# Sixty low-part subtractions change their engine, the weight stream is read further ahead, and two one-hot tables are made earlier in a two-layer decoder kernel

## The chip, the cores and the metric

The kernel runs on one core of one Trainium2 chip. The metric is the device time of one execution in microseconds (us): the median of three runs before the change is 1326.42 us (1326.4 to 1328.45). The core has five engines with queues of their own, each of which works through its instructions in order: TensorE (PE, whose weight loads the profile lists as PEld), VectorE (DVE), ScalarE (ACT), GpSimd (POOL) and SyncE (SP, which here only issues DMAs).

## The reference

The kernel computes two decoder layers on 512 tokens of width 1024. Each layer has a mixer, a cross-attention into 256 memory tokens, and a mixture of 16 experts (hidden width 512), each followed by a layer norm. The change lies in the mixture, cut here to what matters:

```python
def grouped_moe(x, router_w, router_bias, w_gate, w_up, w_down):
    scores = softmax(x @ router_w)                    # 512 x 16
    ...                                               # best of 4 groups, two experts in it
    combine = sum(one_hot(expert_idx) * weights)      # 512 x 16, two entries a token
    y = zeros
    for e in range(16):
        he = silu(x @ w_gate[e]) * (x @ w_up[e])      # 1024 -> 512
        y = y + combine[:, e:e + 1] * (he @ w_down[e])  # 512 -> 1024
    return y

x = layer_norm(ALPHA * x + grouped_moe(x, ...), ln3_g, ln3_b)   # once per layer
```

## The kernel before

**Products in three parts.** Every fp32 number that goes into a product is cut into a high part (rounded to a shorter format) and a low part, the rest. A product is then three matmuls into one PSUM bank: high x high, high x low, low x high (`mm3`, lines 284 to 287, in this order L285, L286, L287). The last of the three needs the low part of the stationary operand, the second the low part of the weights.

**The weight stream.** All weights pass through one stream `W` of 488 pieces of 512 KB. A piece is loaded by a DMA that SP issues (`raw`, L133), ACT copies its high part (`whi`, L153), and then DVE or POOL subtracts: `wlo` = `raw` - `whi` (L156). `on_pool` is the set of pieces whose subtraction stands in POOL's queue. `raw`, `whi`, `wlo` and nearly every other large tile come from one pool of 44 units of 4 KB a partition, which are taken in turn as they come free. `prepare` splits pieces up to MOE_LOOK = 4 ahead of the product that uses them; `pump` issues loads up to `depth` pieces ahead of the split (MOE_DEPTH, an entry for each layer). Inside the expert loops a load also waits until an earlier piece has been split ("a piece is loaded as one is split"), and at most four loads are under way (IN_FLIGHT). Before the loop, beside the router, `moe` issues GATE_DEPTH pieces ahead.

**The expert loops.** An expert has 12 pieces: four of the gate matrix, four of the down matrix, four of the up matrix; the stream holds gate of e+1, down of e, up of e+1. For each expert at most 128 rows of tokens are gathered (`fetch`, a POOL indirect DMA). In one turn e of the loop (L1104 on): DVE forms `h` = silu(gate) x up (L1110); in even turns up to e = 12 DVE makes one-hot tables `r_oh` (L976) for the experts three and four on; PE runs the 24 matmuls of the gate of e+1, and after k = 3 of its eight steps turns `h` (L1117), which ACT (L261) and DVE (L262) split into `hT`, high and low; PE runs the 24 matmuls of the down matrix, with `hT` stationary; `index_of` sums one-hot tables on PE into row numbers (L995, reduced by DVE in L1000 to L1004); ACT scales the result into `ye` (L1149), POOL adds it into DRAM by a scattering DMA (`store`, L1037), and `ye`'s unit is free when that DMA has landed; then the up matrix of e+1. In the last turn of layer 0, DVE makes half of `ye` (L1147); the next layer norm reads the sum back (L1243). In layer 1, the table `oh` of expert 15 (L983), its four transposes (L987) and the ACT copy `back` (L989) are made in turn 9 (TURN_AT) between the store and the up products.

**What sets the order.** The loops stand under a manual schedule for PE, ACT and DVE: these three queues hold the instructions in the order in which the code is written. So a DVE instruction that waits holds up every one written after it. POOL and SP are ordered by the scheduler.

Of the kernel before, what the change touches and what calls it, by code (L numbers as in the profile page):

```python
# [26 lines left out]
NE = 16  # L27
# [6 lines left out]
UNITS = 44  # L34
MM_BANKS = 4
DEPTH = 4
MOE_DEPTH = {"l0_": 16, "l1_": 21}
SHARED = [None, None, False, False]
STAT1 = "VVVA"
BIAS1 = "PPPV"  # L40
TURN_AT = 9
# [2 lines left out]
PLOOK = 1  # L44
NORM_FROM = 4
IN_FLIGHT = 4
GATE_DEPTH = {"l0_": 18, "l1_": 24}
LAST_AHEAD = 1
POOL_W_SPLITS = 2
XO_DEPTH = {"l0_": 18, "l1_": 22}  # L50
# [25 lines left out]
def kernel(ctx: ExitStack, tc: tile.TileContext, I, out, stop=None):  # L76
# [14 lines left out]
    def unit(shape, dt=F32, name="u"):  # L91
        return units.tile(shape, dt, name=name, tag="u")
# [4 lines left out]
    def tpt(name="tp"):  # L97
        return tpp.tile([128, 4, 128], F32, name=name, tag="tp")
# [78 lines left out]
    W = Stream()  # L177
# [32 lines left out]
    plan()  # L210
    first, end = W.span["pool_w"]
    W.on_pool.update(range(first, first + POOL_W_SPLITS))
    for p in ("l0_", "l1_"):
        for e in range(NE - 1):
            W.on_pool.update((W.span[(p, "d", e)][0] + 1, W.span[(p, "u", e + 1)][0]))


    ident = consts.tile([128, 128], F32, name="ident")
# [641 lines left out]
    class Router:  # L860
# [116 lines left out]
                              pos.to_broadcast([128, NT, 128]), op=ALU.is_equal)  # L977
            return oh

        def slots_to_tokens(self, e):  # L980

            oh = unit([128, NT, 128], name="oh")
            vec.tensor_tensor(oh, self.tb.slot[:, None, :].to_broadcast([128, NT, 128]),  # L983
                              self.pos[:, :, e:e + 1].to_broadcast([128, NT, 128]), op=ALU.is_equal)
            tp = tpt()
            for t in range(NT):
                transpose(tp[:, t], oh[:, t], ident)  # L987
            back = unit([128, NT, 128], F32R, name="back")
            act(back, tp, AF.Copy)  # L989
            return back  # L990
# [50 lines left out]
    def expert_rows(w, xT, jobs={}):  # L1041

        ps = mmt()
        for k in range(KC):
            mm3(ps, xT.hi(k), xT.lo(k), *w[k], k == 0, k == KC - 1)
            if k in jobs:
                jobs[k]()
        return ps
# [41 lines left out]
    def experts(r, xT, groups, fetch, turn_part, turned, keep):  # L1090
        p = r.p
        half = lambda n: slice(n * 512, (n + 1) * 512)
        g_ps = expert_rows(W.take((p, "g", 0)), xT)
        r.index([2])
        fetch(2)

        def gate_of():
# [6 lines left out]
        for e in range(NE):  # L1104
# [4 lines left out]
            cur = made["x"]  # L1109
            mul = vec.tensor_tensor(h, h, u_ps, op=ALU.mult)  # L1110
            ohs = [r.one_hot(r.pos[:, :, i:i + 1]) for i in groups.get(e, [])]
            hT = unit([128, 2, 4, 128], F32R, name="hT")

            def turn_h():
# [17 lines left out]
            if not last or not keep:  # L1132
                if e + 2 < NE:
                    made["x"] = Split(128, "xgT")
                for k in range(4):
                    for n in range(2):
                        end = product(n, k)
                    if k == 0 and not last:
                        made["h"] = gate_of()
                    if k == 2 and e + 2 < NE:  # L1140
                        turn_part(e + 2, made["x"], 0)
                if e in groups:
                    r.index_of(groups[e], ohs)
                ye = unit([128, D], name="ye")
                for n in range(2):
                    if n and last:
                        vec.tensor_scalar_mul(ye[:, half(n)], acc[n], scale)  # L1147
                    else:
                        ev = act(ye[:, half(n)], acc[n], AF.Copy, scale=scale)  # L1149
                st = r.store(ye, r.idx[:, e:e + 1])  # L1150
                r.last = [mul, end, ev, st]
                if last:
                    W.after = st
                if e == NE - 2 and keep:
                    ln = Norm(I[p + "ln3_g"], I[p + "ln3_b"])
                    for t in range(NT):
                        nc.gpsimd.dma_start(X[t], r.y_dram[tok(t)])
            else:
                r.yh, r.yl = (unit([128, 2, 512], F32R, name="ye" + i) for i in "hl")
                for n in range(2):  # L1160
                    for k in range(4):
                        end = product(n, k)
                    ev = act(r.yh[:, n], acc[n], AF.Copy, scale=scale)
                    lo = vec.scalar_tensor_tensor(r.yl[:, n], acc[n], scale, r.yh[:, n].bitcast(F32),
                                                  op0=ALU.mult, op1=ALU.subtract)
                r.last = [mul, end, ev, lo, st]
            if not last:
                if e + 3 < NE:
                    fetch(e + 3)
                if e == TURN_AT and keep:  # L1170
                    r.back = r.slots_to_tokens(NE - 1)
                if e == NE - 2:
                    W.last_ahead = W.span[(p, "d", NE - 1)][0] + LAST_AHEAD
                more = {1: lambda: turn_part(e + 2, made["x"], 1)} if e + 2 < NE else {}
                u_ps = expert_rows(W.take((p, "u", e + 1)), cur, more)
# [104 lines left out]
    for layer in range(2):  # L1280
        p = f"l{layer}_"
# [19 lines left out]
        r = Router(p, tb)  # L1301
# [6 lines left out]
        if stop == p + "ln2":  # L1308
            return finish()
        W.depth, W.look = MOE_DEPTH[p], MOE_LOOK  # L1310
        if layer == 0:
# [60 lines left out]
```

## Time and profile before

| | |
|---|---|
| median of three runs | 1326.42 us (1326.4 to 1328.45) |
| profiled execution: its own time, its span | 1327.66 us, 1325.5 us |
| PE, PEld busy | 94%, 79% |
| DVE, ACT, POOL busy | 76%, 58%, 26% |
| expert loop of layer 0 | 404.5 to 684.4 us of the span |
| expert loop of layer 1 | 1008.3 to 1293.2 us of the span |

Busy shares are of the whole span. The numbers of the argument come from stretches, above all the two expert loops. Where a matmul of 128 x 512 has nothing to wait for, the next one starts 0.23 us after it, though each is listed with 0.39 us, since matmuls overlap; so an idle gap of PE in a list of waits is some 0.16 us shorter than the delay between two starts.

### The profile page before, as it was taken

The numbers are of one execution on the slowest core, as the hardware profiler recorded it, in microseconds if no ns is written. First come the engines' busy times: TensorE is split into PE (matmuls) and PEld (weight loads), VectorE is DVE, ScalarE is ACT, GpSimd is POOL, SyncE is SP. The second block draws the span as 40 slices with busy tenths as digits, with TensorE's granted clock in tenths as the row PEclk, the third lists the DMA queues.
The fourth block names the chain that finished last, engine by engine and source line by source line (L and its number), as shares of the span: only waits on it lengthen the run. The fifth ranks groups of instructions, "written<-read, shape, count | busy, mean of one in ns | idle before, by whom it ended". The sixth has DMA issues, their size and how long they took to land. (4 is left out here: it accounts for less than half of the span.)

```text
span 1325.5 us, 18662 instructions
## 1 busy us (share of the span) xinstructions
PE 1248.0 (94%) x6680; PEld 1041.1 (79%) x6680; DVE 1009.3 (76%) x1422; ACT 767.9 (58%) x1143; POOL 347.4 (26%) x231
## 2 busy tenths in 40 slices
PE   7999999999989999999998979999969999989995
PEld 6878989888877777787776868988857778777873
DVE  4784746575769999998876666647659999998985
ACT  4665602463447887778774333246228778777873
POOL 2010001000104544544431320100013344443443
PEclk9999999999989999999999989999969999999999
DMA  9113513247538999999997242207546999999963
GB/s 319 49 49 112 183 56 96 80 143 271 207 107 306 339 354 329 335 347 347 355 356 252 83 139 84 80 17 281 180 155 224 320 355 352 336 354 354 341 223 147
DMA packets 133666, 298.81 MB, mean 225 GB/s; under 512 B 13819, under 2 KB 15883, under 8 KB 133568
## 3 DMA queue, kind: packets, MB, share of 16 engines
q1 hardware_dynamic: 118528, 260.08, 55.0%
q0 software_dynamic: 12160, 27.01, 7.4%
q10 hardware_dynamic: 2880, 10.49, 2.0%
q8 instruction: 53, 0.87, 0.3%
q14 instruction: 45, 0.37, 0.1%
HBM read 287.40 MB, written 26.74 MB: 237 GB/s over the span
## 5 line engine op out<-in xcount | busy, mean ns | idle before, releaser
L156 DVE TENSOR_TENSOR wlo<-raw,whi 128x1024 fp32r<-128x1024 f32 x426 | 576.3, 1391 | 86.9 <-ACT whi L153 64.4
L153 ACT ACTIVATE whi<-raw 128x1024 fp32r<-128x1024 f32 x488 | 488.0, 1058 | 80.8 <-PE mm L286 26.0
L156 POOL TENSOR_TENSOR wlo<-raw,whi 128x1024 fp32r<-128x1024 f32 x62 | 168.0, 2710 | 200.1 <-ACT whi L153 155.5
L285 PE MATMUL mm<-whi,xgTh 128*128 128x512 f32 x512 | 207.7, 406 | 0.0
L286 PE MATMUL mm<-wlo,xgTh 128*128 128x512 f32 x512 | 200.3, 391 | 1.2 <-POOL wlo L156 1.2
L287 PE MATMUL mm<-whi,xgTl 128*128 128x512 f32 x512 | 200.9, 392 | 0.0
L287 PEld LDWEIGHTS mm<-whi,xgTl 128*128 128x128 f32 x512 | 96.5, 188 | 21.4 <-DVE xgTl L262 0.2
L286 PEld LDWEIGHTS mm<-wlo,xgTh 128*128 128x128 f32 x512 | 96.9, 189 | 19.6 <-POOL wlo L156 1.7
L285 PEld LDWEIGHTS mm<-whi,xgTh 128*128 128x128 f32 x512 | 96.7, 189 | 17.6 <-ACT xgTh L261 0.2
L286 PE MATMUL mm<-wlo,hT 128*128 128x512 f32 x256 | 102.7, 401 | 6.4 <-DVE wlo L156 6.2
L349 POOL TENSOR_TENSOR ln_rs<-ln_rs,half_neg 128x1 f32<-128x1 f32 x24 | 31.9, 1331 | 284.0 <-DVE ln_rs L348 284.0
L285 PE MATMUL mm<-whi,hT 128*128 128x512 f32 x256 | 102.6, 401 | 1.4 <-ACT hT L261 1.4
L287 PE MATMUL mm<-whi,hT 128*128 128x512 f32 x256 | 101.9, 398 | 1.3
L1037 POOL DMA_INDIRECT l_y<-ye,r_idx x31 | 65.8, 2122 | 127.9 <-ACT ye L1149 95.7
L261 ACT ACTIVATE xgTh<-tp 128x512 fp32r<-128x512 f32 x64 | 38.2, 600 | 67.3 <-PE tp L271 67.2
L271 PE MATMUL tp<-ident,x 128*128 128x128 f32 x384 | 58.0, 285 | 16.6 <-DMA x<-in_x_dram 6.8
L271 PEld LDWEIGHTS tp<-ident,x 128*128 128x128 f32 x384 | 48.4, 146 | 27.6 <-issue 11.4
L286 PEld LDWEIGHTS mm<-wlo,hT 128*128 128x128 f32 x256 | 48.1, 188 | 24.7 <-DVE wlo L156 16.2
L261 ACT ACTIVATE x1Th<-tp 128x256 fp32r<-128x256 f32 x32 | 12.1, 384 | 86.5 <-PE tp L271 75.9
L285 PE MATMUL mm<-x1Th,whi 128*128 128x256 f32 (+1 forms) x192 | 60.7, 321 | 0.7 <-DVE xqTl L262 0.7
L286 PE MATMUL mm<-x1Tl,whi 128*128 128x256 f32 (+1 forms) x192 | 60.9, 318 | 0.0
L287 PE MATMUL mm<-x1Th,wlo 128*128 128x256 f32 (+1 forms) x192 | 60.9, 318 | 0.0
(328 smaller groups left out, 2616.4 us busy)
## 6 DMA issues: line engine op xcount, KB each, us to landing
raw<-in_l_e_gate_dram SPq DMA_DIRECT2D x128, 512.0 KB
raw<-in_l_e_up_dram SPq DMA_DIRECT2D x128, 512.0 KB
raw<-in_l_e_down_dram SPq DMA_DIRECT2D x128, 512.0 KB
raw<-in_l_xkv_dram SPq DMA_DIRECT2D x32, 512.0 KB
raw<-in_l_w_in_dram SPq DMA_DIRECT2D x22, 512.0 KB
raw<-in_l_w_out_dram SPq DMA_DIRECT2D x16, 512.0 KB
raw<-in_l_xq_dram SPq DMA_DIRECT2D x16, 512.0 KB
raw<-in_l_xo_dram SPq DMA_DIRECT2D x16, 512.0 KB
```

The costliest lines, as they stand in the source:

```text
L153: first = act(hi, raw, AF.Copy)
L156: self.last_split = [first, eng.tensor_sub(lo, raw, hi.bitcast(F32))]
L261: act(hi, src, AF.Copy)
L271: transpose(tp[:, j], rows(c0 + j), ident)
L285: mm(ps, sh, mh, start=first, stop=False)
L286: mm(ps, sh, ml, start=False, stop=False)
L287: return mm(ps, sl, mh, start=False, stop=last)
L349: nc.gpsimd.tensor_tensor(rs[:, 1:2], rs[:, 0:1], half_neg[:, 0:1], op=ALU.pow)
L1037: return nc.gpsimd.indirect_dma_start(out=self.y_dram[:], out_offset=bass.IndirectOffsetOnAxis(ap=idx, axis=0), in_=ye, in_offset=None, bo ...
```

## The change

Four edits. First, the loop that puts two pieces of each expert (the second of down, the first of up) into `on_pool` goes; their 30 subtractions in each loop then stand in DVE's queue, and POOL keeps its DMAs there. Second, MOE_DEPTH of layer 0 goes from 16 to 19 (with the piece being split that is 20 pieces ahead; layer 1 stays at 22), and GATE_DEPTH from 18 and 24 to 24 and 26. Third, the one-hot table for expert 2 is made before the first gate products, and only its sums stay behind them. Fourth, in turn 9 of layer 1 `oh` is made right after `h`, and its transposes and `back` follow the down products; the order on PE stays.

```diff
-MOE_DEPTH = {"l0_": 16, "l1_": 21}
+MOE_DEPTH = {"l0_": 19, "l1_": 21}
-GATE_DEPTH = {"l0_": 18, "l1_": 24}
+GATE_DEPTH = {"l0_": 24, "l1_": 26}
...
     W.on_pool.update(range(first, first + POOL_W_SPLITS))
-    for p in ("l0_", "l1_"):
-        for e in range(NE - 1):
-            W.on_pool.update((W.span[(p, "d", e)][0] + 1, W.span[(p, "u", e + 1)][0]))
...
-        def slots_to_tokens(self, e):
+        def slots(self, e):
             oh = unit([128, NT, 128], name="oh")
             vec.tensor_tensor(oh, ...)
+            return oh
+
+        def to_tokens(self, oh):
             tp = tpt()
...
+        ohs = [r.one_hot(r.pos[:, :, 2:3])]
         g_ps = expert_rows(W.take((p, "g", 0)), xT)
-        r.index([2])
+        r.index_of([2], ohs)
...
             ohs = [r.one_hot(r.pos[:, :, i:i + 1]) for i in groups.get(e, [])]
+            if e == TURN_AT and keep:
+                oh = r.slots(NE - 1)
             hT = unit([128, 2, 4, 128], F32R, name="hT")
...
                 if e in groups:
                     r.index_of(groups[e], ohs)
+                if e == TURN_AT and keep:
+                    r.back = r.to_tokens(oh)
                 ye = unit([128, D], name="ye")
...
-                if e == TURN_AT and keep:
-                    r.back = r.slots_to_tokens(NE - 1)
```

The order on PE and SP is the same before and after. DVE gains 60 subtractions, POOL loses them.

The first place is DVE in the loop of layer 0, from `h` of one turn with one-hot tables to the low part `hT` and what follows; the waits are those that each instruction carries (DMAHW: a load, DMASW: a DMA that POOL issued, Activation: ACT). Before:

```order
L1110 TENSOR_TENSOR h<-h,mm 128x512 [waits DMASW2_49,PE_49]
L976 TENSOR_TENSOR r_oh<-slot,r_pos 128x512 x2
L156 TENSOR_TENSOR wlo<-raw,whi 128x1024 [waits DMAHW6_49,Activation_49]
L262 TENSOR_TENSOR hT<-tp,hT 128x512 [waits Activation_49]
L156 TENSOR_TENSOR wlo<-raw,whi 128x1024 [waits DMAHW0_49,Activation_49]
L156 TENSOR_TENSOR wlo<-raw,whi 128x1024 [waits DMAHW1_49,Activation_49]
L156 TENSOR_TENSOR wlo<-raw,whi 128x1024 [waits DMAHW3_49,DMAHW7_49,Activation_49,Pool_49]
```

And after, in the same turn:

```order
L1112 TENSOR_TENSOR h<-h,mm 128x512 [waits PE_49]
L973 TENSOR_TENSOR r_oh<-slot,r_pos 128x512 x2
L156 TENSOR_TENSOR wlo<-raw,whi 128x1024 [waits DMAHW6_49,Activation_49]
L156 TENSOR_TENSOR wlo<-raw,whi 128x1024 [waits DMAHW7_49,DMASW1_49,Activation_49]
L259 TENSOR_TENSOR hT<-tp,hT 128x512 [waits DVE_49,Activation_49]
L156 TENSOR_TENSOR wlo<-raw,whi 128x1024 [waits DMAHW0_49,Activation_49]
L156 TENSOR_TENSOR wlo<-raw,whi 128x1024 [waits DMAHW1_49,DVE_49,Activation_49]
```

The second down piece has come in ahead of `hT`, and it carries the wait DMASW1: its `wlo` takes the unit of the `ye` of the turn before, which the scattering store still reads. Before, the unit went to a `whi` on ACT that stands behind `hT`:

```order
L261 ACTIVATE hT<-tp 128x512 [waits DVE_49,PE_49]
L153 ACTIVATE whi<-raw 128x1024 [waits DMAHW4_49,DMASW2_49]
L153 ACTIVATE whi<-raw 128x1024 [waits DMAHW5_49,DVE_49]
L153 ACTIVATE whi<-raw 128x1024 [waits DMAHW6_49,DVE_49]
L1099 ACTIVATE h<-mm 128x512 [waits DVE_49,PE_49]
```

These rows of before show ACT in such a turn, where the first `whi` behind `hT` waits for the store (DMASW2).

The second place is DVE in turn 9 of layer 1, from `h` to the table `oh`, before:

```order
L1110 TENSOR_TENSOR h<-h,mm 128x512
L156 TENSOR_TENSOR wlo<-raw,whi 128x1024
L262 TENSOR_TENSOR hT<-tp,hT 128x512
L156 TENSOR_TENSOR wlo<-raw,whi 128x1024 x4
L262 TENSOR_TENSOR xgTl<-tp,xgTh 128x512
L156 TENSOR_TENSOR wlo<-raw,whi 128x1024
L983 TENSOR_TENSOR oh<-slot,r_pos 128x512
```

And after:

```order
L1112 TENSOR_TENSOR h<-h,mm 128x512
L980 TENSOR_TENSOR oh<-slot,r_pos 128x512
L156 TENSOR_TENSOR wlo<-raw,whi 128x1024 x2
L259 TENSOR_TENSOR hT<-tp,hT 128x512
L156 TENSOR_TENSOR wlo<-raw,whi 128x1024 x5
```

`oh` has moved ahead of six subtractions and of `hT`.

The third place is DVE at the start of the loop of layer 0, where `r_oh` is the table of expert 2, before:

```order
L1004 TENSOR_REDUCE r_ws<-idx 128x1 x2
L262 TENSOR_TENSOR xgTl<-tp,xgTh 128x512 x2
L156 TENSOR_TENSOR wlo<-raw,whi 128x1024 x9
L976 TENSOR_TENSOR r_oh<-slot,r_pos 128x512
L1000 TENSOR_REDUCE r_row<-idx 128x1
```

And after:

```order
L1005 TENSOR_REDUCE r_ws<-idx 128x1 x2
L973 TENSOR_TENSOR r_oh<-slot,r_pos 128x512
L259 TENSOR_TENSOR xgTl<-tp,xgTh 128x512 x2
L156 TENSOR_TENSOR wlo<-raw,whi 128x1024 x9
L1001 TENSOR_REDUCE r_row<-idx 128x1
```

The table stood behind nine subtractions and now stands ahead of them.

## Rows read from the trace of the kernel before

**Rows 1.** The head of the profile page: span and engines.

```profile
span 1325.5 us, 18662 instructions
PE 1248.0 (94%) x6680; PEld 1041.1 (79%) x6680; DVE 1009.3 (76%) x1422; ACT 767.9 (58%) x1143; POOL 347.4 (26%) x231
```

**Rows 2.** Stretches of the span: its bounds and length, busy time of PE, PEld, DVE, ACT and POOL with the number of instructions, granted PE clock (1.00 is 2.4 GHz), DMA share, GB/s. The two expert loops, then a part of each, then the end of the first loop.

```profile
404.50:684.40 279.90, 273.01 (x1305) 218.85 (x1305) 258.50 (x242) 219.68 (x265) 132.97 (x60) 1.00 0.97 341
1008.30:1293.20 284.90, 276.15 (x1310) 220.43 (x1308) 270.20 (x243) 217.17 (x266) 124.81 (x60) 0.99 0.93 326
420.00:600.00 180.00, 178.04 (x855) 143.56 (x854) 171.78 (x161) 143.81 (x175) 88.10 (x40) 1.00 0.97 342
1010.00:1190.00 180.00, 175.84 (x846) 140.29 (x844) 176.46 (x159) 140.33 (x173) 80.47 (x39) 1.00 0.96 337
585.00:684.00 99.00, 94.58 (x446) 75.71 (x444) 84.04 (x82) 76.22 (x91) 45.83 (x21) 1.00 0.99 355
```

**Rows 3.** Groups of DVE instructions (count, busy us, mean ns of one, idle time before them), in three stretches: 20 to 380 us, where POOL has next to no subtraction, then 420 to 600 us, then 1010 to 1190 us.

```profile
L156 DVE TENSOR_TENSOR wlo<-raw,whi 128x1024 fp32r<-128x1024 f32 x58 | 68.9, 1220 | 22.3 <-ACT whi L153 15.2 <-issue 7.0
...
L156 DVE TENSOR_TENSOR wlo<-raw,whi 128x1024 fp32r<-128x1024 f32 x98 | 139.4, 1460 | 8.1 <-issue 4.2 <-ACT whi L153 3.9
...
L156 DVE TENSOR_TENSOR wlo<-raw,whi 128x1024 fp32r<-128x1024 f32 x95 | 140.3, 1513 | 3.4 <-ACT whi L153 2.3 <-issue 1.1
```

**Rows 4.** Two source lines: durations in ns (least, median, most), first and last start in us. The one-hot tables over the whole span, POOL's subtractions of the first loop.

```profile
L976 DVE TENSOR_TENSOR r_oh<-slot,r_pos x32: 677/686/2807, 376.1 to 1240.4; 128x512 bf16<-128x512 f32 x32
...
L156 POOL TENSOR_TENSOR wlo<-raw,whi x30: 2373/2683/3477, 406.1 to 675.4; 128x1024 fp32r<-128x1024 f32 x30
```

**Rows 5.** Timeline of turn 2 of the loop of layer 1 (start us, length us, engine, line, idle time before it in brackets): DVE's two tables together, POOL's subtraction beside them, and PE's first and seventh product of the down matrix.

```profile
1047.27 3.02 DVE L976 TENSOR_TENSOR r_oh<-slot,r_pos 128x512 bf16<-128x512 f32 x2
...
1046.75 2.39 POOL L156 TENSOR_TENSOR wlo<-raw,whi 128x1024 fp32r<-128x1024 f32 x1 [3.72 <-DVE wlo L156]
...
1050.85 0.39 PE L285 MATMUL mm<-whi,hT 128*128 128x512 f32 x1
1051.49 0.50 PE L286 MATMUL mm<-wlo,hT 128*128 128x512 f32 x1 [0.25 <-DVE wlo L156]
1052.09 0.50 PE L287 MATMUL mm<-whi,hT 128*128 128x512 f32 x1
...
1054.50 0.39 PE L285 MATMUL mm<-whi,hT 128*128 128x512 f32 x1
1055.33 0.50 PE L286 MATMUL mm<-wlo,hT 128*128 128x512 f32 x1 [0.44 <-DVE wlo L156]
```

**Rows 6.** The same place on PE in turn 2 of the loop of layer 0.

```profile
447.07 0.39 PE L285 MATMUL mm<-whi,hT 128*128 128x512 f32 x1
447.81 0.50 PE L286 MATMUL mm<-wlo,hT 128*128 128x512 f32 x1 [0.36 <-DVE wlo L156]
448.42 0.50 PE L287 MATMUL mm<-whi,hT 128*128 128x512 f32 x1
```

**Rows 7.** PE at the sums of expert 2's table in layer 0 and in layer 1, and at the transposes of `oh`; then the stretch behind these in the columns of rows 2.

```profile
397.95 0.25 PE L995 MATMUL idx<-tokv,r_oh 128*128 128x5 bf16 x4 [1.23 <-DVE r_oh L976]
...
1001.70 0.25 PE L995 MATMUL idx<-tokv,r_oh 128*128 128x5 bf16 x4 [1.91 <-DVE r_oh L976]
...
1192.01 0.63 PE L987 MATMUL tp<-ident,oh 128*128 128x128 f32 x4 [2.83 <-DVE oh L983]
...
1192.50:1196.00 3.50, 3.50 (x13) 2.87 (x12) 1.23 (x1) 1.61 (x3) 0.25 (x1) 0.53 0.98 322
```

**Rows 8.** The end of the first loop (585 to 684 us): ACT's copies as a group, and, earlier, SP's loads (start us, length us) beside the router of layer 0.

```profile
L153 ACT ACTIVATE whi<-raw 128x1024 fp32r<-128x1024 f32 x61 | 62.8, 1061 | 15.5 <-DMA l_y<-ye,r_idx 7.3 <-DMA raw<-in_l_e_up_dram 4.5 <-DMA raw<-in_l_e_down_dram 3.3
...
352.60 38.68 SPq L133 DMA_DIRECT2D raw<-in_l_e_up_dram  x4
392.03 4.81 SPq L133 DMA_DIRECT2D raw<-in_l_e_gate_dram  x4
```

**Rows 9.** The scattering store: ACT's copies behind `hT` in turns 2 and 6 of the first loop, the first down product of turn 6, and the line of the store with the time its DMAs take to land and who waited for it.

```profile
446.11 2.96 ACT L153 ACTIVATE whi<-raw 128x1024 fp32r<-128x1024 f32 x3 [0.99 <-DMA l_y<-ye,r_idx]
...
520.94 2.96 ACT L153 ACTIVATE whi<-raw 128x1024 fp32r<-128x1024 f32 x3 [1.91 <-DMA l_y<-ye,r_idx]
...
520.98 0.39 PE L285 MATMUL mm<-whi,hT 128*128 128x512 f32 x1
...
521.58 0.68 DVE L262 TENSOR_TENSOR hT<-tp,hT 128x512 fp32r<-128x512 f32 x1
...
  ACT whi L153: 17.5, 13
...
DMA to landing us min/median/max: 6.8/9.3/10.7
```

**Rows 10.** From the last product of the first loop to the read-back of its sum.

```profile
691.77 0.39 PE L287 MATMUL mm<-whi,hT 128*128 128x512 f32 x1
...
694.27 1.06 ACT L153 ACTIVATE whi<-raw 128x1024 fp32r<-128x1024 f32 x1 [2.89 <-DMA raw<-in_l_xkv_dram]
...
696.51 0.74 DVE L1147 TENSOR_SCALAR ye<-mm,r_ws 128x512 f32<-128x512 f32 x1
...
704.85 2.00 ACTq L1243 DMA_DIRECT2D x<-l_y  x4
```

**Rows 11.** The second loop's stream: ACT's copies from 1045 to 1265 us as a group.

```profile
L153 ACT ACTIVATE whi<-raw 128x1024 fp32r<-128x1024 f32 x137 | 136.1, 1059 | 3.0 <-DMA l_y<-ye,r_idx 3.0
```

## The prediction

> **What bounds the kernel now.** I read the page first, then a table of stretches, then the groups and timelines of the two expert loops. The page says that PE is busy for 94% of the span and DVE for 76% [rows 1]; an average over stages, so the stretches come next. In both loops PE is busy nearly throughout: 273.0 of 279.9 us and 276.2 of 284.9 [rows 2]. What can be won there is small: 6.9 and 8.7 us of idle PE, plus what matmuls hide of each delay. DVE is close behind (258.5 and 270.2 us), the DMA share is 0.97 and 0.93. So the reader should see three resources near their limit in the same 565 us, and ask for each edit which of the three it relieves and which it loads.
>
> The DVE number is not what it looks like. Where POOL has no subtractions, one `wlo` on DVE takes 1.22 us; in the loops it takes 1.46 and 1.51 on average, over 98 and 95 of them in 180 us [rows 3]. A one-hot table takes 0.68 us alone and 2.8 at most [rows 4], and two of them together took 3.02 us while POOL was in a subtraction that had begun 0.5 us earlier and took 2.39 [rows 5]: the tables stood still until POOL was done. So a part of DVE's busy time is standing still beside POOL: 98 x (1.46 - 1.22) = 24 us of 180 in loop 1 and 95 x (1.51 - 1.22) = 28 in loop 2, the tables not yet counted.
>
> **Part 1: sixty low parts from POOL to DVE.** 30 for each loop, 20 in 180 us. At 1.22 us each, that adds 24 us per 180 to DVE, and what it lost beside POOL (24 and 28, and 1.6 for each pair of tables) goes, for POOL has then only DMAs. DVE's load is about level in loop 1 and some us lower in loop 2; for a whole loop, 30 x 1.22 = 37 us against 40 to 50. That POOL's work was the cause of the long rows is inferred from rows 5; what if it is not is a rival below.
>
> What is won is not load but delay at a few points. In even turns the two tables stand between `h` and the first low parts of the down matrix, and a table blocked by POOL makes these late. In turn 2 of loop 2 the starts 1050.85, 1051.49 and 1052.09 lie 0.64 and 0.60 apart instead of 0.23, and 1054.50 to 1055.33 is 0.83: 0.41 + 0.37 + 0.60 = 1.38 us [rows 5]. In loop 1 it is 0.51 + 0.38 = 0.89 [rows 6]. With tables at 0.68 the low parts come 1.65 us earlier, which is more than each delay. Seven turns of a loop have tables (0 to 12); I count five of them, since the first and the last stand where loads and the loop's start decide: -4.5 us in loop 1, -6.9 in loop 2, and up to two fifths more if all seven count. Odd turns lose nothing now and have no tables; 12 subtractions, `h`, `hT` and two halves of `xgT` are 12 x 1.22 + 4 x 0.68 = 17.4 us in a turn of some 17.8 (280 us over 16, rows 2), so there is cover, but thin.
>
> **Part 2: deeper reading, loop 1.** Two gains and one loss.
>
> The end of loop 1 is short of data. In 585 to 684 us the DMA share is 0.99, ACT's copies wait 4.5 + 3.3 us for loads, and PE idles for 99.0 - 94.6 = 4.4 us, against 2.0 in 180 us (1.1 in 99) before [rows 2, 8]. Loads ran behind use all through the loop, and the stock is gone by the end. Beside the router SP issued only four loads between 352.6 and 391 us [rows 8]: there GATE_DEPTH 24 puts six more pieces, and nothing else loads. Six pieces of 512 KB at 341 GB/s are 9 us of transfers moved out of the loop. Gain: 4.4 - 1.1 = -3.3 us. The last turn gains as well: its last product started at 691.77, but the copy ahead of `ye` on ACT waited for a load until 694.27, and DVE's half of `ye` started at 696.51; the read-back of the sum started at 704.85 [rows 10]. With the load there, `ye` starts when the product ends, about 692.2; 696.5 - 692.0 = -4.5 us, as the store, its landing and the layer norm follow in a chain.
>
> The loss is a new wait. With more raw pieces in the 44 units, the unit that the store of turn e-1 still reads goes to the second down piece's `wlo`, on DVE and now ahead of `hT`; before, a `whi` on ACT behind `hT` took it. Queued behind the waiting `wlo` on DVE are `hT`, for which PE's third down product waits, and everything after. Price: in turn 6 the landing released ACT at 520.94, and the first down product stood at 520.98 [rows 9]. The `wlo` would start at 520.94 and take 1.22, `hT` takes 0.68 [rows 9], and the third product is due two starts behind the first, at 520.98 + 0.45 = 521.43. So 520.94 + 1.22 + 0.68 - 521.43 = 1.41 us. In turn 2 the landing was at 446.11 and the first product at 447.07 [rows 6]: 446.11 + 1.90 - 447.52 = 0.49 us. ACT waited 1.91 and 0.99 us in these two turns and 17.5/13 = 1.35 on average [rows 9], four tenths of the way between, so 0.85 us a turn. A stall in a turn moves the next store by as much, so each turn pays anew: 13 turns, +11 us. Its bounds: nothing, if the store lands 1.45 us or more ahead of the product; 13 x 1.41 = 18 if all turns are like turn 6. Layer 1's depth is unchanged and its freed unit still goes to a piece behind `hT`, so I charge nothing there.
>
> **Part 3: tables ahead of time.** The sums of expert 2's table held PE 1.23 and 1.91 us, the transposes of `oh` 2.83 us [rows 7]. The tables move ahead of 24 gate products, 5.5 us at 0.23, which cover one table (0.68). Behind the wait for `oh` the granted clock was 0.53 for 3.5 us, that is the lower of its two levels (1.2 GHz), after an idle PE; at 0.53 of full speed 3.5 us of work take 1.65 less at the upper level. Gains: -1.2 in loop 1, -1.9 and -2.8 - 1.65 = -4.5 in loop 2. `oh` now stands 0.68 us in front of `hT` in one odd turn, and `back` in front of `ye`; both have cover (up products follow), at most +0.7.
>
> **Sum.** Loop 1: -1.2 - 4.5 - 3.3 - 4.5 + 11 = -2.5. Loop 2: -1.9 - 6.9 - 4.5 = -13.3. Together -15.8 on the profiled execution's 1327.7 us: 1311.9. That execution lies 1.2 us above the median of 1326.4, so 1311.
>
> Loop 2's load side allows this: from 1045 to 1265 us ACT's copies waited 3.0 us, all for stores and none for a load [rows 11].
>
> **Rivals.**
>
> *Better: the new wait costs nothing.* The store lands early enough, since POOL no longer has subtractions and its descriptors are written without sharing with DVE. For it: its landings spread from 6.8 to 10.7 us after the issue with 9.3 as median [rows 9], so 1.4 us earlier is within the rows. Against it: POOL was busy for 133 of 280 us [rows 2], so it was free when about half of the stores came. 1311 - 11 = 1300.
>
> *Transfers bound loop 1 and then loop 2.* If the six pieces do not go out before 391 us, or the loop uses up the stock all the same, -3.3 and -4.5 don't come, and if a faster loop 2 then runs short of loads, it gets perhaps 8 of 13.3: -1.2 - 4.5 + 11 - 8 = -2.7, 1324. For it: DMA shares 0.97 and 0.93. Against it: rows 8's idle queue and rows 11.
>
> *Slower: the new wait costs more.* One mechanism: the store lands later than in before, in every turn of loop 1. From 1.2 us later (15.8/13) the change gains nothing; at 2 us later it adds 26 and gives 1337. For it: landings go up to 10.7, 1.4 above the median, and DVE, which shares something with POOL (rows 5), will be in subtractions when POOL issues a store. The Trainium skill, page "SBUF — State Buffer", section "Who interferes with whom", names this: a DMA whose descriptors GpSimd makes can be starved by VectorE, as they share a port. No run here shows it for this store; a sum by it would be this rival's. Against it: DVE was 92 to 98% busy in before too [rows 2].
>
> *Slower: DVE becomes the bound.* If the long rows have another cause and stay long, 30 x 1.22 more gives 258.5 + 36.6 = 295 in loop 1 and 307 in loop 2, against 279.9 and 284.9: +15 and +22, together +37, less part 3 (-7.6) and the last turn of loop 1 (-4.5): 1351. The Trainium skill, page "Perfetto Trace Analysis", section "Identifying the Most-Contended Engine", takes occupancy as a fair measure of how near VectorE is to its limit, and would speak for this; rows 3 and 5 say that a fifth of this occupancy is standing still.
>
> **How the numbers follow.** Forecast 0.58; better 0.15; transfers 0.13; later store 0.07; DVE bound 0.04; no change for some other reason 0.03. The likeliest's own range is 1303 to 1317 (the wait between 4 and 17 us). With the better rival whole to one side (1300, and 3 us lower if all seven turns of a loop gain) and the transfer rival to the other, 1297 to 1323 leaves out some two in ten. A measurement of this kernel tells 0.2% (2.65 us) from no change: faster is below 1323.8, slower above 1329.1. Faster: 0.58 + 0.15 + 0.10 of the transfer case = 0.83; same: 0.03 of the transfer case and 0.03 for other reasons, 0.06; slower: 0.07 + 0.04 = 0.11.
>
> **What would show it.** Right: `wlo` at 1.22 us in both loops and tables at 0.68; DVE's busy time in the loops not over before; no PE wait at L995 or L987 and a clock of 1.00 behind it; down products of loop 2 at 0.23 apart; in loop 1 a new wait of DVE `wlo` for the scattering store, 13 times, with PE's L287 behind `hT`; no wait for loads after 585 us; `ye` of the last turn right behind its product. Wrong: `wlo` still at 1.4 or more; waits for loads in loop 2; a landing of the store beyond 11 us.

## The result, and the profile after

The changed kernel takes 1308.63 us (median of 4 runs, 1306.69 to 1310.58); the kernel before, with runs on the same chips, 1327.43 (1326.4 to 1330.39). The ratio is 0.9845, 95% interval 0.9825 to 0.9865: 18 to 23 us faster. The four runs lie in two pairs, at 1306.7 and 1307.0 and at 1310.3 and 1310.6 us, and the profiled execution is of the upper one: it took 1310.58 us, its span is 1308.4.

The head of the page, where POOL's share has halved [rows 1]:

```profile
span 1308.4 us, 18639 instructions
PE 1242.6 (95%) x6680; PEld 1042.5 (80%) x6680; DVE 982.5 (75%) x1482; ACT 768.8 (59%) x1143; POOL 170.4 (13%) x171
```

Stretches, in the columns and the order of rows 2:

```profile
402.60:678.20 275.60, 271.77 (x1305) 218.91 (x1304) 250.74 (x272) 221.12 (x265) 40.37 (x30) 1.00 0.97 341
1003.30:1274.10 270.80, 269.80 (x1310) 220.01 (x1308) 251.51 (x273) 217.25 (x266) 40.44 (x30) 1.00 0.97 343
420.00:600.00 180.00, 178.03 (x864) 143.61 (x863) 166.18 (x180) 145.76 (x177) 24.68 (x19) 1.00 0.96 338
1010.00:1190.00 180.00, 180.00 (x882) 146.64 (x881) 168.76 (x185) 146.60 (x181) 27.84 (x20) 1.00 0.98 346
585.00:678.00 93.00, 90.47 (x426) 72.20 (x424) 81.78 (x87) 71.99 (x86) 12.58 (x10) 1.00 0.98 347
```

DVE executes thirty instructions more in each loop and is busy for less: 250.7 us instead of 258.5, and 251.5 instead of 270.2. In loop 2, PE has no idle time left between 1010 and 1190 us; in loop 1 it still has 2.0 us in 180.

The DVE group of low parts in 400 to 600 and in 1010 to 1190 us, as in rows 3, and the one-hot tables' line of rows 4:

```profile
L156 DVE TENSOR_TENSOR wlo<-raw,whi 128x1024 fp32r<-128x1024 f32 x131 | 154.1, 1219 | 14.4 <-ACT whi L153 8.4 <-ACT hT L258 5.4 <-issue 0.2
...
L156 DVE TENSOR_TENSOR wlo<-raw,whi 128x1024 fp32r<-128x1024 f32 x120 | 140.5, 1220 | 9.3 <-ACT whi L153 8.2 <-DMA raw<-in_l_e_down_dram 0.9
...
L973 DVE TENSOR_TENSOR r_oh<-slot,r_pos x32: 681/685/692, 376.7 to 1222.9; 128x512 bf16<-128x512 f32 x32
```

In the two loops not one low part or table is long any more: the longest low part took 1.23 us, and the longest table 0.692 where it took 2.807.

To see where the time went, this table follows five milestones: the turning of `h` on PE in the first and the last turn of each loop, and the end. It holds for all kernels run, so that the experiments can be read from it too (us of the profiled spans).

| kernel | to turn 0, loop 1 | loop 1, turns 0 to 15 | between | loop 2, turns 0 to 15 | to the end | ratio to before |
|---|---|---|---|---|---|---|
| before | 407.3 | 277.1 | 326.6 | 282.2 | 32.4 | 1 |
| changed | 405.4 | 272.9 | 327.7 | 268.1 | 34.3 | 0.9845 |
| e1 low parts alone | 407.6 | 273.5 | 328.0 | 272.1 | 32.4 | 0.9901 |
| e2 reading alone | 407.0 | 297.6 | 326.8 | 282.0 | 34.1 | 1.0109 |
| e3 tables alone | 405.9 | 278.2 | 325.6 | 277.7 | 32.4 | 0.9936 |
| e4 changed, without low parts | 405.8 | 292.3 | 327.0 | 276.5 | 32.3 | 1.0066 |
| e5 changed, without reading | 405.5 | 275.6 | 324.4 | 268.1 | 32.4 | 0.9848 |
| e6 changed, depth 21 | 405.9 | 273.1 | 324.2 | 268.1 | 34.3 | 0.9821 |
| e7 changed, depth 18 | 406.5 | 271.9 | 324.9 | 268.1 | 32.4 | 0.9848 |
| e8 changed, GpSimd again | 405.6 | 305.3 | 325.6 | 296.5 | 32.3 | 1.029 |
| e9 changed, ye first | 406.8 | 272.2 | 323.1 | 268.7 | 32.4 | 0.979 |
| e10 depth 18, ye first | 405.7 | 272.5 | 321.4 | 268.2 | 34.2 | 0.9788 |
| e11 depth 21, ye first | 405.5 | 273.0 | 323.7 | 268.2 | 32.4 | 0.9806 |
| e12 without reading, ye first | 405.8 | 276.6 | 318.7 | 268.2 | 32.4 | 0.9813 |

Of the changed kernel's 17.1 us of span, loop 2 gave 14.1 and loop 1 gave 4.2, the start 1.9; between the loops 1.1 were lost and at the end 1.9.

Loop 2, turn 2, at the place of rows 5, DVE and then PE:

```profile
1041.39 1.29 DVE L973 TENSOR_TENSOR r_oh<-slot,r_pos 128x512 bf16<-128x512 f32 x2
1042.60 2.35 DVE L156 TENSOR_TENSOR wlo<-raw,whi 128x1024 fp32r<-128x1024 f32 x2
1044.87 0.69 DVE L259 TENSOR_TENSOR hT<-tp,hT 128x512 fp32r<-128x512 f32 x1
...
1045.02 0.39 PE L282 MATMUL mm<-whi,hT 128*128 128x512 f32 x1
1045.25 0.39 PE L283 MATMUL mm<-wlo,hT 128*128 128x512 f32 x1
1045.61 0.50 PE L284 MATMUL mm<-whi,hT 128*128 128x512 f32 x1
```

Two tables take 1.29 us instead of 3.02, and the second product follows the first after 0.23 us; the third, which needs `hT`'s low part, is 0.13 late.

Loop 1 has the new wait. DVE in turns 1 and 7, PE's second and third down product of turn 7, the stores of turns 0 and 6 on POOL, and two lines from the store's source line:

```profile
422.69 1.22 DVE L156 TENSOR_TENSOR wlo<-raw,whi 128x1024 fp32r<-128x1024 f32 x1
425.11 1.23 DVE L156 TENSOR_TENSOR wlo<-raw,whi 128x1024 fp32r<-128x1024 f32 x1 [1.20 <-ACT hT L258]
426.25 0.68 DVE L259 TENSOR_TENSOR hT<-tp,hT 128x512 fp32r<-128x512 f32 x1
...
535.03 1.23 DVE L156 TENSOR_TENSOR wlo<-raw,whi 128x1024 fp32r<-128x1024 f32 x1 [1.84 <-ACT whi L153]
536.17 0.68 DVE L259 TENSOR_TENSOR hT<-tp,hT 128x512 fp32r<-128x512 f32 x1
...
536.16 0.39 PE L283 MATMUL mm<-wlo,hT 128*128 128x512 f32 x1
536.91 0.50 PE L284 MATMUL mm<-whi,hT 128*128 128x512 f32 x1 [0.36 <-DVE hT L259]
...
416.25 1.65 POOL L1038 DMA_INDIRECT l_y<-ye,r_idx  x1 [17.11 <-DVE r_row L1001]
...
525.52 1.58 POOL L1038 DMA_INDIRECT l_y<-ye,r_idx  x1 [16.43 <-DVE wlo L156]
...
L1038 POOL DMA_INDIRECT l_y<-ye,r_idx x31: 1550/1600/1892, 416.2 to 1269.7; - x31
...
DMA to landing us min/median/max: 6.1/8.8/9.9
```

DVE stands idle for 1.20 and 1.84 us before the second down piece's low part, ahead of `hT`. The list puts the wait down to ACT, which had written `whi` well before. The two low parts start 8.86 and 9.51 us after the issue of the store of the turn before, which is where landings lie (6.1 to 9.9); that it is the landing, as the waits in the order say, was also tested (e2, e6, e7). PE's third product then came 0.52 us late in turn 7. The store itself has become quicker: POOL needs 1.60 us for it (median; 2.24 in the trace of before), and it lands 8.8 us after the start of its issue instead of 9.3 [rows 9].

The end of loop 1, to hold against rows 10: the last product, ACT, DVE's half of `ye`, and the read-back.

```profile
685.58 0.39 PE L284 MATMUL mm<-whi,hT 128*128 128x512 f32 x1
...
687.93 1.06 ACT L153 ACTIVATE whi<-raw 128x1024 fp32r<-128x1024 f32 x1 [2.85 <-DMA raw<-in_l_xkv_dram]
689.23 1.06 ACT L153 ACTIVATE whi<-raw 128x1024 fp32r<-128x1024 f32 x1 [0.24 <-DMA raw<-in_l_xkv_dram]
690.19 0.67 ACT L1155 ACTIVATE ye<-mm,r_ws 128x512 f32<-128x512 f32 x1
...
691.46 0.75 DVE L1153 TENSOR_SCALAR ye<-mm,r_ws 128x512 f32<-128x512 f32 x1
...
699.74 1.77 ACTq L1247 DMA_DIRECT2D x<-l_y  x4
```

The last product comes 6.2 us sooner than before, but `ye` only 5.05 (691.46 against 696.51): ACT still stands idle for 2.85 us before a copy that waits for a load.

### The profile page after: what moved, and what is told of

It is laid out like the page before. It is cut to its first block, busy times and chain, and to the rows that moved or that the text cites. A ratio compares the mean times of both kernels' runs of the same rounds, so it can differ in the third digit from the quotient of the medians.

```text
span 1308.4 us, 18639 instructions
## 1 busy us (share of the span) xinstructions
PE 1242.6 (95%) x6680; PEld 1042.5 (80%) x6680; DVE 982.5 (75%) x1482; ACT 768.8 (59%) x1143; POOL 170.4 (13%) x171
## 5 line engine op out<-in xcount | busy, mean ns | idle before, releaser
L1038 POOL DMA_INDIRECT l_y<-ye,r_idx x31 | 49.8, 1606 | 473.3 <-ACT ye L1155 209.4
L284 PE MATMUL mm<-whi,hT 128*128 128x512 f32 x256 | 103.5, 404 | 3.3 <-DVE hT L259 3.3
L282 PE MATMUL mm<-whi,hT 128*128 128x512 f32 x256 | 103.7, 405 | 1.4 <-ACT hT L258 1.4
L284 PEld LDWEIGHTS mm<-whi,hT 128*128 128x128 f32 x256 | 48.7, 190 | 21.2 <-DVE hT L259 11.3
```

The source lines that it names most:

```text
L282: mm(ps, sh, mh, start=first, stop=False)
L284: return mm(ps, sl, mh, start=False, stop=last)
L1038: return nc.gpsimd.indirect_dma_start(out=self.y_dram[:], out_offset=bass.IndirectOffsetOnAxis(ap=idx, axis=0), in_=ye, in_offset=None, bo ...
```

## The experiments

Twelve kernels ran, each against runs of the kernel before on the same chip. e1 to e4 take the change apart; e5 to e8 test the two claims about waits; e9 to e12 test the end of loop 1.

**e1, low parts alone.**

```diff
     W.on_pool.update(range(first, first + POOL_W_SPLITS))
-    for p in ("l0_", "l1_"):
-        for e in range(NE - 1):
-            W.on_pool.update((W.span[(p, "d", e)][0] + 1, W.span[(p, "u", e + 1)][0]))
```

> The kernel before with the sixty low parts on VectorE and nothing else changed. If GpSimd's subtractions were what made VectorE's rows long, every low part takes 1.22 us in both loops, two one-hot tables take 1.3 us together instead of 3.0, the delays at the down products of even turns go, and the run is 12 to 14 us faster than before, with 10 or more of it in the loop of layer 1. If the long rows have another cause, they stay at 1.46 to 1.51, VectorE needs about 295 and 307 us for the loops, and the run is 10 us or more slower.

Measured: 1315.9 us, ratio 0.9901 (0.9876 to 0.9926), 13 us. Loop 2 is 10.1 us shorter, loop 1 3.6. Low parts in 1010 to 1190 us:

```profile
L156 DVE TENSOR_TENSOR wlo<-raw,whi 128x1024 fp32r<-128x1024 f32 x118 | 138.1, 1218 | 9.9 <-ACT whi L153 8.1 <-DMA raw<-in_l_e_down_dram 1.1 <-DMA raw<-in_l_e_gate_dram 0.3
```

As expected in size and place. Both loops' even turns drop to 18.4 us here, as long as loads are ahead: ACT's copies behind `hT` still wait for the store in six turns of loop 1, but no down product does. From turn 9 on, loop 1 has long turns (20.9 us at most).

**e2, deeper reading alone.**

```diff
-MOE_DEPTH = {"l0_": 16, "l1_": 21}
+MOE_DEPTH = {"l0_": 19, "l1_": 21}
-GATE_DEPTH = {"l0_": 18, "l1_": 24}
+GATE_DEPTH = {"l0_": 24, "l1_": 26}
```

> The kernel before with the deeper reading (19 and 24, 26) alone; the low parts stay on GpSimd. My theory: the six pieces read beside the router reach the end of loop 1, but the unit of the scattered ye now goes to a subtraction on GpSimd (second down piece), which waits for the landing and then takes 2.4 us; gain and loss are about equal, within 4 us of before. Rival: reading further ahead is what made loop 1 faster, and this run is 5 us or more faster than before, with all of it ahead of the loop of layer 1.

Measured: 1344.65 us, ratio 1.0109 (1.0079 to 1.0138): slower by 15 us in the medians; in the profiled execution loop 1 is 20.5 us longer and loop 2 unchanged. I had expected gain and loss to be level; the loss is far larger. Turn 2 of loop 1, POOL and PE, and POOL's subtractions of that loop:

```profile
448.31 6.12 POOL L156 TENSOR_TENSOR wlo<-raw,whi 128x1024 fp32r<-128x1024 f32 x2 [7.88 <-ACT whi L153]
...
449.34 0.39 PE L285 MATMUL mm<-whi,hT 128*128 128x512 f32 x1
452.14 0.75 PE L286 MATMUL mm<-wlo,hT 128*128 128x512 f32 x1 [2.41 <-POOL wlo L156]
...
L156 POOL TENSOR_TENSOR wlo<-raw,whi x29: 2377/3282/4464, 405.8 to 688.2; 128x1024 fp32r<-128x1024 f32 x29
```

POOL's subtraction now cannot start before the unit is free: in turns 1, 2 and 4 to 7 it starts 9.0 to 10.3 us after the issue of the store of the turn before, as landings do. It then takes 3.28 us (median; 2.68 before, rows 4), and PE stands 2.41 us in front of its result. Turns 2 to 10 with tables take 22.2 us where they took 19.2.

**e3, tables alone.**

```diff
+        ohs = [r.one_hot(r.pos[:, :, 2:3])]
         g_ps = expert_rows(W.take((p, "g", 0)), xT)
-        r.index([2])
+        r.index_of([2], ohs)
...
+            if e == TURN_AT and keep:
+                oh = r.slots(NE - 1)
...
+                if e == TURN_AT and keep:
+                    r.back = r.to_tokens(oh)
```

> The kernel before with the two one-hot tables made ahead alone. By the trace: 1.2 and 1.9 us at the sums of expert 2, 2.8 us at the transposes in turn 9 and 1.65 us of low clock behind them, together 7.6 us faster, of which 6.4 from the sums of layer 1 on. If the tables are only late for another reason (VectorE's queue as a whole), the waits stay at half their size or more and the run is at most 3 us faster.

Measured: 1321.09 us, ratio 0.9936 (0.9915 to 0.9957), 8.5 us. Loop 2 is 4.5 us shorter, the first milestone comes 1.4 sooner, the stretch between is 1.0 shorter, and loop 1 is 1.1 longer, so the profiled span is only 5.6 us shorter. The gain and its places are as expected; the 1.1 us were not.

**e4, the change without the low parts.**

```diff
     W.on_pool.update(range(first, first + POOL_W_SPLITS))
+    for p in ("l0_", "l1_"):
+        for e in range(NE - 1):
+            W.on_pool.update((W.span[(p, "d", e)][0] + 1, W.span[(p, "u", e + 1)][0]))
```

> The changed kernel with the thirty low parts of each loop back on GpSimd: deeper reading and early tables only. If the parts add up, it is slower than the changed kernel by what the low parts are worth, 11 to 14 us, so 5 to 8 us faster than before; turns of the loop of layer 1 last 19.7 us again where they have tables. If the low parts are worth little by themselves, it stands within 4 us of the changed kernel.

Measured: 1336.88 us, ratio 1.0066 (1.0042 to 1.009). Neither: it is slower than before. The parts do add up (1.0109 x 0.9936 = 1.0044), but the low parts are worth 28 us in the company of the deeper reading and 13 without it.

**e5, the change without deeper reading.**

```diff
-MOE_DEPTH = {"l0_": 19, "l1_": 21}
+MOE_DEPTH = {"l0_": 16, "l1_": 21}
-GATE_DEPTH = {"l0_": 24, "l1_": 26}
+GATE_DEPTH = {"l0_": 18, "l1_": 24}
```

> The changed kernel without the deeper reading (16, and 18 and 24 beside the router). By the first four runs low parts and tables alone give 0.990 x 0.994 = 0.984 of before, which is what the whole change gave (0.9845). If so, the deeper reading is worth nothing in the sum: this run stands within 3 us of the changed kernel, its loop of layer 1 lasts 268 us as there, and in its loop of layer 0 the waits for loads at the end (some 4 us) stand in the place of the waits behind the scattering store (some 4.7 us). If the reading helps, it is 4 us or more slower than the changed kernel.

Measured: 1308.98 us, ratio 0.9848 (0.9827 to 0.987), the same as the whole change. Loop 1 is 2.7 us longer than in the changed kernel. ACT's copies in 585 to 684 us:

```profile
L153 ACT ACTIVATE whi<-raw 128x1024 fp32r<-128x1024 f32 x61 | 64.0, 1062 | 18.5 <-DMA raw<-in_l_e_down_dram 12.9 <-DMA raw<-in_l_e_gate_dram 1.9 <-DMA raw<-in_l_e_up_dram 1.8
```

Waits for loads are 16.6 us there, against 7.8 before [rows 8], presumably because loop 1, with DVE faster, uses up its stock sooner (e1, at the same depth, has 13.4). So the deeper reading removes a lack of loads and puts a wait for the store in its place.

**e6, depth 21 in layer 0.**

```diff
-MOE_DEPTH = {"l0_": 19, "l1_": 21}
+MOE_DEPTH = {"l0_": 21, "l1_": 21}
```

> The changed kernel with depth 21 instead of 19 in layer 0: the unit of the scattered ye then goes to a raw piece, so SyncE and no engine waits for the landing. If the unit is what matters, no down product of loop 1 waits for hT, and the turns with and without tables last 18.4 and 17.75 us as in layer 1, some 4.7 us less in all; the run is 2 to 5 us faster than the changed kernel, if the loads at the loop's end don't take it back. If the waits come from a late VectorE, they stay.

Measured: 1306.04 us, ratio 0.9821 (0.9803 to 0.9839), so perhaps 3 us faster than the changed kernel, though the intervals overlap. The waits of DVE behind the store are gone up to turn 13, but loop 1 is not shorter (273.1 us): from turn 1 to turn 10 a pair of turns lasts 37.0 us, as these rows of PE show (553.58 to 572.52 and 535.52 to 553.58 are 18.9 and 18.1 us). Behind them are two lines from the list of waits in 420 to 600 us (us in total, times, longest).

```profile
535.52 0.63 PE L1121 MATMUL tp<-ident,h 128*128 128x128 f32 x4 [0.24 <-DVE h L1112]
553.58 0.63 PE L1121 MATMUL tp<-ident,h 128*128 128x128 f32 x4 [0.16 <-DVE h L1112]
572.52 0.63 PE L1121 MATMUL tp<-ident,h 128*128 128x128 f32 x4 [0.26 <-DVE h L1112]
...
ACT whi L153 <- PE mm L284: 13.6, 34, 0.8
...
PE tp L1121 <- DVE h L1112: 2.0, 10, 0.3
```

24 pieces of 512 KB in 37.0 us are 340 GB/s, which is what the loops reach [rows 2]. That the loads set this pace is a guess, and this trace speaks against it: in 420 to 600 us neither PE nor ACT waits for a load, and DVE does once, for 1.0 us. What PE waits for most, at all ten turnings, is `h`. ACT's copies wait 34 times for a matmul, 13.6 us in all, where the changed kernel has 10 such waits and 5.0 us: with two more pieces loaded ahead, a copy may have to wait for a unit that a product still reads. That too is an inference; no run here separates the two.

**e7, depth 18 in layer 0.**

```diff
-MOE_DEPTH = {"l0_": 19, "l1_": 21}
+MOE_DEPTH = {"l0_": 18, "l1_": 21}
```

> The changed kernel with depth 18: now hT itself takes the unit of the scattered ye, so its high part on ScalarE and its low part on VectorE both wait for the landing, and the first down product with them. If the landing is what is waited for, the wait is longer than in the changed kernel, 1 to 2 us a turn, 13 times, and the run 10 to 20 us slower than the changed kernel, with the loop of layer 1 unchanged at 268 us. If a piece fewer in hand is of no weight by itself and the unit neither, it stands within 2 us of the changed kernel.

Measured: 1306.12 us, ratio 0.9848 (0.982 to 0.9876). I was wrong by the whole amount. The wait is there, on ACT, in eleven turns (list of waits, 400 to 690 us):

```profile
ACT hT L258 <- DMA l_y<-ye,r_idx: 28.1, 11, 3.4
```

It is longer than DVE's wait at depth 19, 2.6 us each, and yet the turns until 533 us last 18.4 and 17.75 us, like those of loop 2. Here only `hT`'s two halves stand behind the landing, some 1.3 us; at depth 19 it is a low part of 1.22 us and then `hT`'s low half. The length of a wait says little; what counts is what stands between its end and the product.

**e8, GpSimd does its old subtractions again, into a scrap tile.**

```diff
                 self.last_split = [first, eng.tensor_sub(lo, raw, hi.bitcast(F32))]
+                if i in self.again:
+                    for c in range(4):
+                        part = lambda t: t.rearrange("p a n -> p (a n)")[:, c * 256:(c + 1) * 256]
+                        nc.gpsimd.tensor_sub(scrap, part(raw[:]), part(hi[:].bitcast(F32)))
```

> The changed kernel, and GpSimd does the thirty subtractions of each loop over again, in four quarters each, into a scrap tile that nobody reads; VectorE still makes all low parts. If VectorE's long rows come from GpSimd working beside it, they come back: low parts at 1.45 us or more on average instead of 1.22, tables up to 2.8 us, VectorE over its limit, and the run 15 us or more slower than the changed kernel. If the gain was only that VectorE makes a low part in 1.2 us where GpSimd needs 2.4 to 2.7, the rows stay at 1.22 us and the run within 3 us.

Measured: 1367.06 us, ratio 1.029 (1.027 to 1.031), 58 us slower than the changed kernel. Low parts and tables in 1010 to 1190 us, and DVE and POOL side by side in one turn of loop 2 (line numbers are shifted by the edit):

```profile
L157 DVE TENSOR_TENSOR wlo<-raw,whi 128x1024 fp32r<-128x1024 f32 x101 | 137.2, 1409 | 4.6 <-POOL scrap L161 2.5 <-ACT whi L154 2.0
...
L982 DVE TENSOR_TENSOR r_oh<-slot,r_pos 128x512 bf16<-128x512 f32 x11 | 9.2, 870 | 0.0
...
1099.62 7.94 DVE L157 TENSOR_TENSOR wlo<-raw,whi 128x1024 fp32r<-128x1024 f32 x5
...
1094.62 13.54 POOL L161 TENSOR_TENSOR scrap<-raw,whi 128x256 f32<-128x256 f32 x8 [0.30 <-issue]
```

Five low parts take 7.94 us beside POOL, 1.59 each, and eight quarters on POOL take 13.54, 1.69 each. So work on POOL whose result nobody reads slows DVE by its mere presence, and DVE slows POOL. The quarters are a heavier load than the old subtractions (they alone take 99 us in these 180, of which loop 2 takes up 153, where all of POOL's work took 80 before, rows 2, and DVE waited 2.5 us in the same stretch for units that they still read), so the 58 us are no measure of the old cost; the direction is shown.

**e9, `ye` first in the last turn of layer 0.**

```diff
             if last:
-                W.last_ahead = 1 << 30
+                W.last_ahead = 1 << 30 if keep else W.span[(p, "d", e)][1]
                 turn_h()
...
                 if last:
                     W.after = st
+                    W.last_ahead = 1 << 30
```

> The changed kernel, and in the last turn of layer 0 no piece of the next weights is split before ye: its two halves no longer stand behind copies that wait for loads. In the changed kernel the last product started at 685.6 us and VectorE's half of ye at 691.5. If the copies ahead of it are what holds it, ye starts within 1 us of the last product, the read-back of the sum comes some 5 us sooner, TensorE idles less before the next transposes, and the run is 3 to 7 us faster than the changed kernel. If the landing of the store is hidden behind other work, the time stays.

Measured: 1302.18 us, ratio 0.979 (0.9761 to 0.9819), 6.4 us faster than the changed kernel by the medians; the two intervals don't touch. ACT, DVE and the read-back:

```profile
686.06 0.69 ACT L1155 ACTIVATE ye<-mm,r_ws 128x512 f32<-128x512 f32 x1 [2.92 <-PE mm L284]
...
686.74 0.75 DVE L1153 TENSOR_SCALAR ye<-mm,r_ws 128x512 f32<-128x512 f32 x1 [1.97 <-PE mm L284]
...
697.31 2.02 ACTq L1248 DMA_DIRECT2D x<-l_y  x4
```

`ye` now waits for the product alone. The read-back comes 2.4 us sooner, not the 5 expected, though loop 1 ended 0.7 later; on ACT it stands behind the `v` of the next stage (696.15 us). In the profiled spans the stretch between the loops is 4.6 us shorter than in the changed kernel. This is the version that beats both kernels.

**e10 to e12, the same with depth 18, with depth 21, and without deeper reading.** Each has e9's edit, and:

```diff
-MOE_DEPTH = {"l0_": 19, "l1_": 21}
+MOE_DEPTH = {"l0_": 18, "l1_": 21}   # e10; 21 in e11, 16 in e12
...
-GATE_DEPTH = {"l0_": 24, "l1_": 26}
+GATE_DEPTH = {"l0_": 18, "l1_": 24}  # e12 alone
```

> Depth 18 in layer 0 together with ye ahead of the next pieces. By the runs at 18 (0.985 of before) and the term for ye (5 us, 0.0038): 0.981 of before, some 3 to 7 us faster than the changed kernel. If the two overlap, because both are short of loads, no better than ye first alone.

> Depth 21 in layer 0 together with ye ahead of the next pieces. At depth 21 a pair of turns took 37.0 us for 24 pieces, which is the pace of the loads (24 x 512 KB at 341 GB/s is 36.9 us). If the loads bound loop 1 there, it still lasts 273 us, and the gain is that of ye alone: 0.982 - 0.0038 = 0.978 of before.

> Low parts and tables without the deeper reading (16, 18 and 24), with ye ahead of the next pieces. If the deeper reading matters once ye doesn't wait for the loads of the next weights, this is 3 us or more slower than the changed kernel with ye first; if reading ahead is without weight here too, the two are within 2 us.

Measured: 1303.62 us, 0.9788 (0.976 to 0.9817); 1304.58, 0.9806 (0.9778 to 0.9833); 1303.82, 0.9813 (0.9782 to 0.9844). None is told apart from e9. Between the loops the edit takes off 4.6 us at depth 19 (e9), 3.5 at 18 (e10 against e7) and 5.7 without deeper reading (e12 against e5), but only 0.5 at depth 21 (e11 against e6), by one profile each; why so little there is not shown. Loop 1 lasts 273.0 us at depth 21, as expected, which does not tell whether loads or units hold it. Without the deeper reading, loop 1 is 4.4 us longer than in e9, and the stretch between is 4.4 shorter: what the loads lack in the loop is there behind it.

## Why the prediction was right, point by point

Forecast 1311 from 1326.4, 15.8 us; measured 18.8 by the medians, and the time lies in the range. The sum came out better than its terms, and that is in part luck: two of them were wrong by some 6 and 7 us, in opposite directions. Sorted into the columns of the table, the forecast was -1.2 us up to turn 0 of loop 1, +3.2 in loop 1, -6.4 between the loops, -11.4 in loop 2 and nothing at the end; the profiled spans have -1.9, -4.2, +1.1, -14.1 and +1.9.

- *Low parts from POOL to DVE, delays at the down products.* Right in mechanism, and shown: e1 removes the long rows, e8 brings them back without giving DVE a single low part less. In loop 2 turns 2, 4, 6, 8 and 10 became 1.35, 1.42, 1.35, 1.39 and 1.20 us shorter, 6.7 together where 6.9 stood. The turns that I left out gave 2.4 more (the first 0.8, the last three 1.6). In loop 1, where 4.5 stood, the same five turns became 3.5 us shorter in e1. The rival with DVE as the bound fell: 250.7 and 251.5 us.
- *Deeper reading, the end of loop 1 short of loads: -3.3 and -4.5.* The first came roughly: waits of ACT's copies for loads in 585 to 684 us fell from 7.8 to 4.1, though only four of the six pieces went out early (from 305 to 390 us SP issued 23 pieces instead of 19). The second failed: "With the load there, `ye` starts when the product ends". The load was not there. The pieces that ACT's copies wait for ahead of `ye` are those of the next stage, and while the loop's last product came 6.2 us sooner, the last of these copies came only 5.0 sooner (689.23 against 694.27), after waits of 2.85 and 0.24 us, where before there was one of 2.89. From the product to DVE's half of `ye` it is 5.9 us now and was 4.7, so the term came out as +1.1. This is half of what the transfer rival said. The remedy is not to read earlier but not to stand behind the load (e9).
- *The new wait: +11.* Right in place and cause (e2, e6 and e7), wrong in size. Against the turns of loop 2, turns 1 to 13 of loop 1 are 4.2 us longer in all; 3.7 of it is the later start of PE's third down product, 0.28 us a turn where 0.85 stood. DVE waited visibly in ten of these turns, not in thirteen. Two steps were wrong. The 13 waits and 17.5 us of rows 9 are those of the whole span: 3.0 us of them are in loop 2 [rows 11], and loop 1 had eleven. And the landing was taken from the trace of before. There it came 0.04 to 1.08 us ahead of the first down product, in the eleven turns in which ACT waited for it; here it came 0.34 to 1.54 us ahead, in the ten, and by the prediction's own sum 1.45 us ahead is enough to cost nothing. The store takes 0.6 us less to issue, which is a part of the landing that comes 0.5 us sooner. The median landing is 8.5 to 8.8 us where the low parts have left POOL (the changed kernel, e1, e5) and 9.2 or 9.3 where they have not (before, e2, e4); in e8, where POOL subtracts again, it is 8.8, so why it is sooner stays open. This is a part of the better rival.
- *Deeper reading as a whole.* My three terms sum to +3.2 us; e5 says 0 within some 4 us. The whole gain of the change is that of the low parts and the tables: 0.9901 x 0.9936 = 0.9838.
- *Tables.* -7.6 us forecast, 8.5 measured alone by the medians and 5.6 by the profiled spans (e3). In the changed kernel turn 9 of loop 2 became 4.9 us shorter (4.5 forecast), and PE waits for none of the tables that were moved.
- *What I had not counted: the clock*, which cost some 2.4 us between the loops and, in the profiled execution, 1.9 at the end, below.
- *Two slips in the sums.* 280 us over 16 turns are 17.5 us, not 17.8, and from 692.2 to 696.5 it is 4.3 us, not 4.5; neither moves the forecast by more than 0.2.

The later store as a slower rival did not come: it landed 9.9 us after its issue at most. Starvation of its descriptors by DVE, the rule of the Trainium skill quoted in the prediction ("SBUF — State Buffer", "Who interferes with whom"), does not show here: with thirty more subtractions on DVE in each loop, landings became quicker.

## What to carry to other kernels

An engine that is off the critical path can still hold up one that is on it by its presence: look for a group whose mean is longer in one stretch than in another, and at what runs beside it. Before a pool of buffers is filled deeper, ask which instruction takes the unit that a slow transfer still holds, on which engine, and what is queued behind it; here the same depth change cost some 15 us or nothing, depending on the engine that had to wait. And when work is prepared ahead in an ordered queue, see that it doesn't put a wait for data of the next stage ahead of the last result of this one.

## What the runs showed of the hardware

TensorE's clock took back a part of the gain. Stretches around the layer norm behind loop 1, of the changed kernel and then of e9, in the columns of rows 2:

```profile
701.00:707.80 6.80, 2.28 (x11) 1.56 (x10) 4.77 (x8) 0.00 (x0) 1.47 (x1) 0.92 0.80 302
707.80:714.20 6.40, 6.39 (x21) 5.35 (x22) 4.31 (x8) 1.04 (x3) 1.45 (x1) 0.55 0.73 243
```

```profile
700.00:707.00 7.00, 7.00 (x37) 5.89 (x36) 6.39 (x11) 0.38 (x1) 2.12 (x2) 1.00 0.69 224
707.00:714.00 7.00, 6.58 (x33) 4.86 (x31) 5.71 (x12) 4.78 (x11) 0.81 (x1) 1.00 0.96 337
```

In the changed kernel PE was busy for 2.3 of 6.8 us while it waited for the norm, and then had a granted clock of 0.55, near the lower level (1.2 GHz), for the next 6.4 us; the second group of transposes started 2.7 us sooner than before (714.15 against 716.85), where the read-back had been 5.1 sooner. In e9 PE was busy for 13.6 of these 14.0 us and the clock stayed at 1.00. The kernel before had a low stretch near by as well, but there PE had to wait 2.85 us for the norm behind it, so it cost little:

```profile
701.00:706.00 5.00, 5.00 (x17) 3.92 (x16) 0.00 (x0) 0.00 (x0) 0.00 (x0) 0.66 0.40 65
```

At the very end, the stretch behind loop 2 is either 32.4 or some 34.2 us long in all these kernels (the last but one column of the table). The first 6.8 us of it, in the changed kernel and in e7:

```profile
1274.10:1280.90 6.80, 5.42 (x16) 3.62 (x17) 4.19 (x4) 3.43 (x4) 2.15 (x4) 0.69 0.52 180
```

```profile
1271.50:1278.30 6.80, 5.04 (x18) 2.92 (x19) 4.19 (x4) 3.65 (x5) 2.14 (x4) 1.00 0.48 154
```

The same instructions, with the same waits on PE at first (0.78 us for `h`, 0.69 for `hT`), and a granted clock of 0.69 in one and 1.00 in the other. Which execution gets the lower clock there was not found out; the two values are 1.8 us apart, about half of the 3.9 us over which the changed kernel's four runs spread.
